# Attention block pipeline of a two-layer trunk: earlier weight splits, one slot for a short block's maps, later low parts, earlier fetches

## The chip, the cores and the metric

One Trainium2 chip, one of its cores. The metric is the device time of one launch in microseconds, the median of several runs. The engines are named as the profile names them: PE (TensorE, matrix products, its weight loads are PEld), DVE (VectorE), ACT (ScalarE), POOL (GpSimd) and SP (SyncE, which here issues every DMA). Each engine takes its own instructions strictly in the order in which they were written, and waits at the first one whose inputs are not there.

## The reference, cut to what matters

Two layers over 1024 tokens of width 1024: a gated short convolution, then causal differential attention with 8 heads of two maps each.

```python
proj = h @ w_in                                   # D -> 4 W: q, k, v, z
logits = einsum('bqhd,bkhd->bhqk', q_blk, k) * scale + bias      # causal, blocks of 128 queries
p = softmax(logits).reshape(bsz, N_DIFF_HEADS, 2, Q_BLOCK, s)
a = p[:, :, 0] - lam * p[:, :, 1]                 # the two maps of a head
o = rmsnorm(einsum('bhqk,bkhe->bqhe', a, v), subln_g) * (1 - lambda_init)
x = x + (o * silu(z)) @ w_out                     # then a final rmsnorm
```

## The kernel before, in words

Products are made from halves: a float32 operand is split into a high part (a rounded copy) and a low part (what is left), and three products of 128x128 by 512 or 256 columns take the place of one. A weight **unit** of 128x1024 is loaded by SP into a raw slot (`wr`, two slots), ACT writes its high part `wh` (L407), POOL subtracts to get its low part `wl` (L408); there are two slots of each, and a raw slot is free again when POOL has subtracted.

The second layer is what the change touches. It runs in 64 **steps**, s = 8h + qb, head h and block qb of 128 queries; the eight steps of a head are a **round** here. In step s, PE computes the scores of block s (`scores`, L612), then the product of one half unit (`half.mm`, L132 for keys, queries and gates, L525 for values), then, at even s, the values of the blocks s-4 and s-3 (`values`, L659). DVE adds the bias and takes the maximum (L615, L617), ACT writes the two maps' exponentials (L619); one step later `differences` subtracts the maps on DVE (L633), ACT and DVE, or for qb >= 5 ACT and POOL (L640), make the 16-bit high and low part, and SP transposes both by DMA (L645) for the value product. The first map lies in a slot of `r_p1` (five slots), the second in one of `r_p2` (three); the second holds the two 16-bit parts, so that it is free again only when its transposition has landed.

The table `plan` says which half unit a step multiplies; `when` gives the step in which a unit is split, as soon as the unit before the last is used up, and `loads` the step in which its raw weights are fetched. Inside a step the order is: loads, evictions (`evict`), squares of a finished half head, the first part of the last half unit's eviction (`first`), scores, splits of weights (`preps`), the product, `differences` of the block before, the rest.

After a head's half is done, its 512 norm factors are stored to HBM as single elements (`store_factors`, L688) and fetched back, spread over all partitions, as `rb` (`fetch_factors`, L692, a tile of 128x512 in one slot `dgl`); POOL multiplies them and the gate into the head's output two steps into the next round but one (L494, `Gate.multiply`), and stores that (L496). In the last eight steps `closing` also fetches, scales and splits the output weights (L854 to L856), with the subtraction on DVE; `tail` then does the output projection.

Of the kernel before, what the change touches and what calls it, by code (L numbers as in the profile page):

```python
# [50 lines left out]
def trunk(ctx: ExitStack, tc: tile.TileContext, a: dict, out: bass.AP):  # L51
# [539 lines left out]
    def scores(h, qb):  # L591
# [5 lines left out]
        p1_ = r_p1.tile([P, S], F32, name="p1")  # L597
        p2_ = r_p2.tile([P, S], F32, name="p2")
# [23 lines left out]

    def differences(h, qb):

        hd = heads[h]
        L = (qb + 1) * P
        p1_, p2_, st = hd.pop(("p", qb))

        cs = sm.tile([P, 2], F32, tag="cs", bufs=2, name="cs")
        V.reciprocal(out=cs, in_=st)  # L630
        V.tensor_scalar(out=cs[:, 1:2], in0=cs[:, 1:2], scalar1=st[:, 0:1], scalar2=nlam, op0=ALU.mult, op1=ALU.mult)
        V.tensor_scalar(out=cs[:, 0:1], in0=cs[:, 0:1], scalar1=cc, scalar2=None, op0=ALU.mult)
        V.scalar_tensor_tensor(out=p1_[:, :L], in0=p2_[:, :L], scalar=cs[:, 1:2], in1=p1_[:, :L],  # L633
                               op0=ALU.mult, op1=ALU.add)
        p16 = p2_.bitcast(F16)
        ah, al = p16[:, :L], p16[:, L:2 * L]
        if qb >= 5:
            A.activation(out=p1_[:, :L], in_=p1_[:, :L], func=AF.Copy, scale=cs[:, 0:1])
            A.activation(out=ah, in_=p1_[:, :L], func=AF.Copy)
            G.tensor_tensor(out=al, in0=p1_[:, :L], in1=ah, op=ALU.subtract)  # L640
        else:
            A.activation(out=ah, in_=p1_[:, :L], func=AF.Copy, scale=cs[:, 0:1])  # L642
            V.scalar_tensor_tensor(out=al, in0=p1_[:, :L], scalar=cs[:, 0:1], in1=ah, op0=ALU.mult, op1=ALU.subtract)  # L643
        at = p1_.bitcast(F16).rearrange("p (b q) -> p b q", q=P)
        dma(out=at[:, :2 * qb + 2, :], in_=p16[:, :2 * L], transpose=True)  # L645
        hd["at", qb] = at
# [42 lines left out]

    def fetch_factors(h, half):  # L690
        rbs[h, half] = rb = sm.tile([P, 512], F32, tag="dgl", name="rb")
# [29 lines left out]
    add("q", 1, (4, 7))  # L721
    add("k", 1, (5, 6))
# [12 lines left out]
    loads, preps, when = {}, {}, {}  # L735
    for i, (_, _, u) in enumerate(units):
        when[i] = max(units[i - 2][1] + 1, when[i - 1], -1) if i > 1 else -9
        preps.setdefault(when[i], []).append(u)
        loads.setdefault(max(when[i - 2] + 1, -1) if i > 1 else -9, []).append(u)

    fetches = {}
    for t, half in plan.items():
        if isinstance(half, Gate) and half.h < L7:
            fetches.setdefault(t - 1 + half.half, []).append((half.h, half.half))

    def step(s, score=True):
        h, qb = divmod(s, 8)
        for u in loads.get(s, ()):
            u.load()
# [5 lines left out]
        if s % 4 == 3 and 0 <= s - 7:  # L755
            ph, pqb = divmod(s - 7, 8)
            sqo = ph, pqb // 4, head_squares(ph, pqb // 4)
        if last:
            last.first()
        half = plan.get(s)  # L760
# [86 lines left out]
    def prep_w(d):  # L847
# [8 lines left out]
        V.tensor_tensor(out=wl, in0=wr, in1=f(wh), op=ALU.subtract)  # L856
# [80 lines left out]
    def layer1():  # L937
        prelude()
        for s in range(NS):
            step(s)  # L940
# [3 lines left out]

    def closing(s):

        if s == 56:
            n = r_q.n
            q0, q1, q2, q3, spare = (r_q.tags[(n + 1 + i) % 5] for i in range(5))
            r_raw.append(Ring(sl, [spare, (wp, "wr0"), (wp, "wr1")]))  # L950
            pb = [r_p2.tags[(r_p2.n + i) % 3] for i in (1, 2, 0)]
            wtags.update({2: r_v.tags[:2], 3: (q0, q1), 4: (r_k.tags[1], pb[0]), 5: (q2, q3), 6: r_k.tags[2:],
                          7: (pb[1], pb[2])})
            fetch_w(2)
        elif s == 57:
            prep_w(2)
        elif s == 59:
            fetch_w(3)
            fetch_w(0)
        elif s == 60:  # L960
            prep_w(3)
            prep_w(0)
        elif s == 61:
            yh[:], yl[:] = new_x()
            fetch_y(0, 0)
            fetch_y(2, 0)
        elif s == 62:
            splits(0, 0)
            fetch_w(1)
            fetch_y(4, 0)  # L970
        elif s == 63:
            splits(2, 0)
            differences(L7, 7)
            for d in (0, 2, 3):
# [131 lines left out]
```

## Time and profile before

| | us |
|---|---|
| median of 3 runs (1184.52 to 1190.43) | 1188.75 |
| the profiled execution's own time | 1192.76 |
| its span, first to last instruction | 1191.0 |
| first layer and the start of the second, to the scores of step 0 | 490.9 |
| rounds 0 to 6 (steps 0 to 55) | 477 |
| round 7 (steps 56 to 63) to the end of its products, and the tail | 223 |
| PE busy | 1090.4 |

The steps can be found in the timeline by PE's score products (L612): four instructions for a block under 4, eight for the others. A stretch between two such places is a step or a round, and the view of busy time by stretches gives for it, after its bounds and length, the busy time of PE, PEld, DVE, ACT and POOL (with the number of instructions) and the clock that PE was granted (1.00 is 2.4 GHz, 0.50 is 1.2 GHz), then the DMA engines' share and GB/s. A matmul's end is modelled, so that PE's busy time in a stretch at half clock is longer for the same work.

### The profile page before, as it was taken

The page shows a single profiled execution, that of the slowest core. Times are in us where ns is not written, and L with a number is a line of the kernel's source. Part 1 is how long each engine was busy: PE and PEld are TensorE (multiplying, and loading weights), DVE is VectorE, ACT ScalarE, POOL GpSimd, SP SyncE. Part 2 cuts the span into 40 slices and gives each one's busy share as a digit, 9 for nine tenths or more (in the row PEclk, how much of TensorE's full clock was granted, in tenths as well). Part 3 has the DMA queues.
Part 4 walks back from the last instruction along what each step waited for, and adds up shares of the span by engine and source line. Part 5 has one row for each costly group of instructions (what it writes and reads, how often), then busy time and mean ns, then how long its engine had stood idle before and what let it go on. Part 6 is the DMA issues. An engine that isn't in the chain of part 4 may idle for free.

```text
span 1191.0 us, 15198 instructions
## 1 busy us (share of the span) xinstructions
PE 1090.4 (92%) x5900; PEld 916.7 (77%) x5900; DVE 598.1 (50%) x951; ACT 437.1 (37%) x715; POOL 517.2 (43%) x315
## 2 busy tenths in 40 slices
PE   8899999999999999798799898989989895878886
PEld 6678888888888888776678787888878785666686
DVE  6563323222324223678485766767676564762522
ACT  3221111111112322447254563746455362544421
POOL 7553433424424443454246564545546461131143
PEclk9899999999999999889799998999999897888898
DMA  5211111111113341434467685886767774453132
GB/s 180 86 55 54 53 39 50 54 53 38 52 53 100 131 145 71 97 92 105 67 84 119 111 155 83 134 131 97 121 92 141 104 143 63 113 136 107 62 107 80
DMA packets 123192, 111.86 MB, mean 94 GB/s; under 512 B 88128, under 2 KB 95984, under 8 KB 123120
## 3 DMA queue, kind: packets, MB, share of 16 engines
q1 hardware_dynamic: 123120, 110.90, 42.4%
q8 instruction: 46, 0.75, 0.3%
q14 instruction: 26, 0.21, 0.1%
HBM read 67.82 MB, written 11.59 MB: 67 GB/s over the span
## 4 chain that ended last, share of the span: by engine, by line
PE 59%; DVE 11%; POOL 8%; issue 7%; DMA 7%; ACT 6%; SPq 1%; POOLq 0%; DVEq 0%; ACTq 0%
PE big L132 35%; PE mm L132 18%; POOL wl L408 3%; PE sc L612 2%; DVE nm L617 2%; DMA wr<-in_w_in 2%; DMA p<-p 2%; PE av L659 2%; DMA wr<-in_w_out 2%; DVE p L633 1%; PE mm L525 1%; DMA qt<-qt 1%; POOL o L494 1%; POOL qt L465 1%; ACT wh L407 1%
## 5 line engine op out<-in xcount | busy, mean ns | idle before, releaser
L132 PE MATMUL mm<-xh,wl 128*128 128x512 f32 (+1 forms) x424 | 170.0, 401 | 20.3 <-POOL wl L408 20.3
L120 POOL TENSOR_TENSOR wl<-wr,wh 128x1024 fp32r<-128x1024 f32 x37 | 90.1, 2435 | 215.9 <-ACT wh L119 215.9
L132 PE MATMUL mm<-xl,wh 128*128 128x512 f32 (+1 forms) x424 | 169.2, 399 | 4.7 <-DVE xl L826 4.7
L132 PE MATMUL mm<-xh,wh 128*128 128x512 f32 (+1 forms) x424 | 169.3, 399 | 2.2 <-ACT xh L825 2.0
L408 POOL TENSOR_TENSOR wl<-wr,wh 128x1024 fp32r<-128x1024 f32 x40 | 95.6, 2392 | 129.5 <-ACT wh L407 129.0
L132 PE MATMUL big<-xh,wh 128*128 128x512 f32 x472 | 147.2, 391 | 2.2 <-DVE cr L289 2.2
L119 ACT ACTIVATE wh<-wr 128x1024 fp32r<-128x1024 f32 x37 | 39.2, 1061 | 294.4 <-PE big L132 293.6
L132 PE MATMUL big<-xh,wl 128*128 128x512 f32 x472 | 146.8, 391 | 0.0
L132 PE MATMUL big<-xl,wh 128*128 128x512 f32 x472 | 146.4, 390 | 0.0
L619 ACT ACTIVATE p<-sc,nm 128x256 f32<-128x256 f32 (+7 forms) x128 | 94.4, 740 | 90.1 <-DVE nm L617 33.6
L132 PEld LDWEIGHTS mm<-xh,wl 128*128 128x128 f32 x424 | 83.9, 198 | 41.9 <-POOL wl L408 25.3
L612 PE MATMUL sc<-kt,qt 128*128 128x512 f32 (+2 forms) x384 | 91.6, 374 | 16.6 <-ACT p L619 13.0
L132 PEld LDWEIGHTS big<-xh,wh 128*128 128x128 f32 x472 | 89.0, 189 | 21.0 <-issue 2.6
L132 PEld LDWEIGHTS big<-xl,wh 128*128 128x128 f32 x472 | 88.9, 188 | 18.6
L132 PEld LDWEIGHTS big<-xh,wl 128*128 128x128 f32 x472 | 88.9, 188 | 18.4
L132 PEld LDWEIGHTS mm<-xl,wh 128*128 128x128 f32 x424 | 83.9, 198 | 22.4 <-DVE xl L826 6.9
L132 PEld LDWEIGHTS mm<-xh,wh 128*128 128x128 f32 x424 | 83.9, 198 | 19.0 <-ACT xh L825 3.5
L617 DVE TENSOR_REDUCE nm<-sc 128x2 f32<-128x256 f32 (+5 forms) x96 | 92.0, 958 | 3.3
L612 PEld LDWEIGHTS sc<-kt,qt 128*128 128x128 f32 x384 | 67.4, 201 | 27.7 <-ACT p L619 16.1
L525 PE MATMUL mm<-wl,xh 128*128 128x256 f32 x256 | 75.4, 294 | 7.0 <-POOL wl L408 7.0
L643 DVE SCALAR_TENSOR_TENSOR p<-p,cs,p 128x128 f16<-128x128 f32 (+4 forms) x40 | 46.9, 1174 | 68.6 <-ACT p L642 68.1
L525 PE MATMUL mm<-wh,xh 128*128 128x256 f32 x256 | 75.5, 295 | 0.8 <-DVE tq L460 0.6
(186 smaller groups left out, 2038.8 us busy)
## 6 DMA issues: line engine op xcount, KB each, us to landing
wr<-in_w_in SPq DMA_DIRECT2D x53, 512.0 KB, 3.7
wr<-in_w_out SPq DMA_DIRECT2D x16, 512.0 KB, 4.7
wr<-in_w_v SPq DMA_DIRECT2D x16, 512.0 KB, 5.1
qt<-qt SPq DMA_DIRECT2D x32, 256.0 KB, 7.5
xr<-in_xT SPq DMA_DIRECT2D x15, 512.0 KB, 4.3
x2d<-x SPq DMA_DIRECT2D x8, 512.0 KB, 2.8
kt<-lo SPq DMA_DIRECT2D x32, 128.0 KB, 9.5
rb<-rrd SPq DMA_DIRECT2D x14, 256.0 KB, 5.4
```

The lines of the kernel that those rows point to most:

```text
L119: A.activation(out=wh, in_=wr, func=AF.Copy)
L120: G.tensor_tensor(out=wl, in0=wr, in1=f(wh), op=ALU.subtract)
L132: T.matmul(ps[:, o:o + n], lhsT=w[:, s], rhs=r[k][:, t:t + n], start=(k == 0 and r is rh and w is wh), stop=(k == KC - 1 and w is wl))
L407: A.activation(out=self.wh, in_=self.wr, func=AF.Copy)
L408: G.tensor_tensor(out=self.wl, in0=self.wr, in1=f(self.wh), op=ALU.subtract)
L465: G.tensor_tensor(out=qt[own[m], 1, :], in0=tq[own[m]], in1=f(qt)[own[m], 0, :], op=ALU.subtract)
L525: T.matmul(self.pts[tp][:, i, :], lhsT=x[k][:, ts], rhs=w[:, kk], start=(k == 0 and i == 0 and x is xh and w is wh), stop=(k == KC - 1 and ...
L612: T.matmul(sc[:, i, c0:c1_], lhsT=qt[:, var, ts], rhs=kt[:, c0:c1_], start=(var == 0), stop=(var == 1))
L617: V.tensor_reduce(out=nm[:, ms], in_=sc[:, :, :L], axis=AX, op=ALU.max, negate=True)
L619: A.activation(out=(p1_, p2_)[m][:, :L], in_=sc[:, i, :L], func=AF.Exp, bias=nm[:, m:m + 1], accum_out=st[:, m:m + 1])
L643: V.scalar_tensor_tensor(out=al, in0=p1_[:, :L], scalar=cs[:, 0:1], in1=ah, op0=ALU.mult, op1=ALU.subtract)
L659: T.matmul(av[:, qi * P:(qi + 1) * P], lhsT=v[:, kb, es], rhs=at[:, r, :], start=(kb == 0 and r == 0 and v is vh), stop=(kb == qb and v is ...
```

## The change

It changes no arithmetic and no shape; the order of PE's instructions stays the same but for the swap of two units in round 0. It does five things:

1. A unit whose split falls in the step right ahead of its use (`soon`) is split first in that step (`early`), before evictions and scores; the raw loads move behind `first` in the step, and a load that follows an early split stands in the same step and not in the next. In round 0 the keys of head 1 come before its queries.
2. Blocks with qb < 4 put both maps into one `r_p1` slot (two halves of 512), and use no `r_p2` slot.
3. For qb >= 5 POOL's low part and the transposition (`turn`) are put off into the next step, ahead of `first`.
4. The factors of both halves of a head are fetched in the same step, one step ahead of the gate's first product, into one `r_p2` slot.
5. In the last round the output weights and finished heads are fetched ahead of the step (`opening`) and not after it, and POOL takes the subtraction of three of the weights from DVE.

```diff
@@ scores
-        p1_ = r_p1.tile([P, S], F32, name="p1")
-        p2_ = r_p2.tile([P, S], F32, name="p2")
+        if qb < 4:
+            p12 = r_p1.tile([P, 2, 512], F32, name="p1")
+            p1_, p2_ = p12[:, 0, :], p12[:, 1, :]
+        else:
+            p1_ = r_p1.tile([P, S], F32, name="p1")
+            p2_ = r_p2.tile([P, S], F32, name="p2")
@@ differences
-            G.tensor_tensor(out=al, in0=p1_[:, :L], in1=ah, op=ALU.subtract)
...
+        def turn():
+            if qb >= 5:
+                G.tensor_tensor(out=al, in0=p1_[:, :L], in1=ah, op=ALU.subtract)
+            at = p1_.bitcast(F16).rearrange("p (b q) -> p b q", q=P)
+            dma(out=at[:, :2 * qb + 2, :], in_=p16[:, :2 * L], transpose=True)
+            hd["at", qb] = at
+        if qb < 5 or (h, qb) == (0, 7):
+            turn()
+        else:
+            turns.append(turn)
@@ fetch_factors
-        rbs[h, half] = rb = sm.tile([P, 512], F32, tag="dgl", name="rb")
+        if h == L7 - 1:
+            rb = sm.tile([P, 512], F32, tag="dgl", name="rb")
+        elif half:
+            rb = rb2[0][:, 1, :]
+        else:
+            rb2[:] = [r_p2.tile([P, 2, 512], F32, name="rb")]
+            rb = rb2[0][:, 0, :]
+        rbs[h, half] = rb
@@ tables
-    add("q", 1, (4, 7))
-    add("k", 1, (5, 6))
+    add("k", 1, (4, 6))
+    add("q", 1, (5, 7))
...
-        preps.setdefault(when[i], []).append(u)
-        loads.setdefault(max(when[i - 2] + 1, -1) if i > 1 else -9, []).append(u)
+        soon[i] = when[i] > 0 and use == when[i] + 1
+        (early if soon[i] else preps).setdefault(when[i], []).append(u)
+        loads.setdefault(max(when[i - 2] + (not soon[i - 2]), -1) if i > 1 else -9, []).append(u)
...
-        if isinstance(half, Gate) and half.h < L7:
+        if isinstance(half, Gate) and half.h < L7 - 1:
+            fetches.setdefault(t - 1 - half.half, []).append((half.h, half.half))
+        elif isinstance(half, Gate) and half.h < L7:
             fetches.setdefault(t - 1 + half.half, []).append((half.h, half.half))
@@ step
-        for u in loads.get(s, ()):
-            u.load()
+        for u in early.get(s, ()):
+            u.prep()
...
+        for fn in turns:
+            fn()
+        turns.clear()
         if last:
             last.first()
+        for u in loads.get(s, ()):
+            u.load()
@@ prep_w
-    def prep_w(d):
+    def prep_w(d, eng=V):
-        V.tensor_tensor(out=wl, in0=wr, in1=f(wh), op=ALU.subtract)
+        eng.tensor_tensor(out=wl, in0=wr, in1=f(wh), op=ALU.subtract)
@@ layer1, closing
+            if s >= 56:
+                opening(s)
             step(s)
...
-    def closing(s):
+    def opening(s):
...
             fetch_w(2)
-        elif s == 57:
-            prep_w(2)
         elif s == 59:
             fetch_w(3)
             fetch_w(0)
-        elif s == 60:
-            prep_w(3)
-            prep_w(0)
         elif s == 61:
-            yh[:], yl[:] = new_x()
             fetch_y(0, 0)
             fetch_y(2, 0)
         elif s == 62:
+            fetch_w(1)
+        elif s == 63:
+            fetch_y(4, 0)
+
+    def closing(s):
...
+        elif s == 57:
+            prep_w(2, G)
+        elif s == 60:
+            prep_w(3, G)
+            prep_w(0, G)
...
         elif s == 62:
             splits(0, 0)
-            fetch_w(1)
-            fetch_y(4, 0)
```

The order of instructions shows it at two places. The first is POOL's queue in round 4 (from step 32 on), `wl` being a weight's low part, `p` a map's low part, `o` the gate and factor products. Before:

```order
L408 TENSOR_TENSOR wl<-wr,wh 128x1024
L640 TENSOR_TENSOR p_6406<-p_6405,p_6406 128x1024
L494 TENSOR_TENSOR o<-o,rb 128x512
L494 TENSOR_TENSOR o<-o,th 128x512
L408 TENSOR_TENSOR wl<-wr,wh 128x1024
L494 TENSOR_TENSOR o<-o,rb 128x512
L494 TENSOR_TENSOR o<-o,th 128x512
L408 TENSOR_TENSOR wl<-wr,wh 128x1024
L678 TENSOR_TENSOR rr<-rr,neghalf 128x4
L408 TENSOR_TENSOR wl<-wr,wh 128x1024
```

And now:

```order
L408 TENSOR_TENSOR wl<-wr,wh 128x1024
L652 TENSOR_TENSOR p_7105<-p_7104,p_7105 128x1024
L494 TENSOR_TENSOR o<-o,rb 128x512
L494 TENSOR_TENSOR o<-o,th 128x512
L408 TENSOR_TENSOR wl<-wr,wh 128x1024
L494 TENSOR_TENSOR o<-o,rb 128x512
L494 TENSOR_TENSOR o<-o,th 128x512
L408 TENSOR_TENSOR wl<-wr,wh 128x1024 x2
L691 TENSOR_TENSOR rr<-rr,neghalf 128x4
```

The queue up to the keys' split (the third `wl`) stands as it stood; the queries' split, which stood behind the factor's root `rr`, now follows the keys' directly.

The second is SP's queue of the same places, from a round's step 6 into the next round: `rb` is the fetch of factors, `rrd` their store, `wr` raw weights, a DMA_TRANSPOSE of 12, 14 and 16 the blocks 5, 6 and 7 of a head. Before:

```order
L645 DMA_TRANSPOSE p_6250<-p_6251 128x12x128
L697 DMA bias<-stripd 128x2x256
L437 DMA kt<-lo 64x512 x2
L645 DMA_TRANSPOSE p_6316<-p_6317 128x14x128
L692 DMA rb<-rrd 128x512
L403 DMA wr<-in_w_v 128x1024
L466 DMA qt<-qt 64x2x512 x2
L645 DMA_TRANSPOSE p_6405<-p_6406 128x16x128
L688 DMA rrd<-rr 128x4x1
```

And now:

```order
L719 DMA bias<-stripd 128x2x256
L654 DMA_TRANSPOSE p_6227<-p_6228 128x12x128
L437 DMA kt<-lo 64x512
L403 DMA wr<-in_w_v 128x1024
L437 DMA kt<-lo 64x512
L714 DMA rb<-rrd 128x512 x2
L654 DMA_TRANSPOSE p_6293<-p_6294 128x14x128
L466 DMA qt<-qt 64x2x512 x2
L701 DMA rrd<-rr 128x4x1
L654 DMA_TRANSPOSE p_6388<-p_6389 128x16x128
```

Both fetches of factors now stand ahead of block 6's transposition, and block 7's transposition behind the single-element store and no longer ahead of it.

## Rows read from the trace of the kernel before

**Rows 1.** Rounds 1 to 6: length, engines' busy time, PE's granted clock.

```profile
554.90:625.60 70.70, 56.87 (x366) 49.32 (x366) 48.18 (x86) 35.31 (x67) 29.09 (x18) 0.88 0.53 79
625.60:695.20 69.60, 64.91 (x415) 55.97 (x414) 43.96 (x81) 36.41 (x65) 37.38 (x23) 0.95 0.71 126
695.20:763.70 68.50, 64.31 (x415) 55.41 (x415) 49.13 (x90) 37.43 (x70) 35.51 (x24) 0.95 0.71 105
763.70:829.30 65.60, 61.62 (x414) 53.64 (x413) 43.37 (x81) 34.99 (x63) 36.48 (x23) 1.00 0.81 129
829.30:897.80 68.50, 63.94 (x415) 54.97 (x414) 48.82 (x90) 38.46 (x72) 36.40 (x24) 0.98 0.68 113
897.80:967.90 70.10, 64.64 (x415) 55.79 (x414) 43.43 (x81) 35.33 (x63) 36.71 (x23) 0.95 0.72 121
```

**Rows 2.** Waits of PE over the span: total us, times, longest.

```profile
PE mm L132 <- POOL wl L408: 20.3, 9, 5.2
PE sc L612 <- ACT p L619: 13.0, 8, 5.4
PE cps L157 <- ACT sqo L668: 12.0, 1, 12.0
```

**Rows 3.** Timeline, POOL and PE, step 36: start, us, idle before, releaser.

```profile
795.16 1.30 POOL L494 TENSOR_TENSOR o<-o,rb 128x512 f32<-128x512 f32 x1 [9.26 <-DMA rb<-rrd]
...
797.96 2.34 POOL L408 TENSOR_TENSOR wl<-wr,wh 128x1024 fp32r<-128x1024 f32 x1
...
800.36 0.50 PE L132 MATMUL mm<-xh,wl 128*128 128x512 f32 x1 [3.37 <-POOL wl L408]
```

**Rows 4.** Line view: the stores of factors, and transpositions in rounds 2 to 6.

```profile
L688 SPq DMA_DIRECT2D rrd<-rr x14: 520/578/935, 571.7 to 1021.6; - x14
...
DMA to landing us min/median/max: 9.9/10.0/11.0
...
L645 SPq DMA_TRANSPOSE p<-p x40: 1177/1332/3923, 630.3 to 961.1; - x40
...
DMA to landing us min/median/max: 3.1/5.2/13.4
```

**Rows 5.** Timeline, ACT and PE, steps 11 and 12.

```profile
588.24 0.69 ACT L619 ACTIVATE p<-sc,nm 128x512 f32<-128x512 f32 x1 [8.94 <-DMA p<-p]
...
589.07 0.69 PE L612 MATMUL sc<-kt,qt 128*128 128x384 f32 x1 [5.41 <-ACT p L619]
```

**Rows 6.** Timeline, ACT and PE, step 59.

```profile
995.88 1.15 ACT L854 ACTIVATE wr<-wr,gsub 128x1024 f32<-128x1024 f32 x1 [15.33 <-DMA wr<-in_w_out]
...
1009.33 1.87 PE L157 MATMUL cps<-ones_r,sqo 128*128 128x1 f32 x8 [12.01 <-ACT sqo L668]
```

**Rows 7.** Busy time by stretches: steps 10, 12, 36, 59, 60 and 61.

```profile
557.25:575.26 18.01, 12.62 (x106) 11.87 (x103) 11.65 (x17) 9.28 (x22) 12.17 (x7) 0.81 0.55 89
582.83:601.30 18.47, 10.53 (x45) 8.38 (x45) 7.95 (x16) 6.14 (x11) 7.14 (x5) 0.72 0.33 93
795.20:806.00 10.80, 7.43 (x43) 5.93 (x42) 6.92 (x15) 5.36 (x10) 8.60 (x6) 1.00 0.48 140
990.70:1011.00 20.30, 8.29 (x40) 6.81 (x37) 10.94 (x15) 6.64 (x11) 5.01 (x3) 0.73 0.26 62
1011.00:1021.40 10.40, 10.20 (x43) 8.37 (x43) 7.83 (x19) 5.07 (x11) 2.22 (x2) 0.70 0.46 147
1021.40:1030.50 9.10, 7.07 (x35) 5.60 (x32) 5.79 (x8) 5.93 (x7) 0.61 (x1) 1.00 0.22 33
```

**Rows 8.** Timeline, SP and PE, round 4: block 7's transposition and its value product.

```profile
776.59 2.46 SPq L645 DMA_TRANSPOSE p<-p  x1
...
785.03 2.69 PE L659 MATMUL av<-p,vt 128*128 128x128 f16 x45
```

**Rows 9.** Timeline, DVE: L643 of 384 columns beside a POOL split, and alone.

```profile
590.56 2.29 DVE L643 SCALAR_TENSOR_TENSOR p<-p,cs,p 128x384 f16<-128x384 f32 x1 [9.31 <-ACT p L642]
...
1013.15 0.62 DVE L643 SCALAR_TENSOR_TENSOR p<-p,cs,p 128x384 f16<-128x384 f32 x1 [1.04 <-ACT p L642]
```

More of the change, by code (lines that the diff above doesn't have):

```diff
@@ L621, in scores @@
         hd["p", qb] = p1_, p2_, st
+    turns = []
     def differences(h, qb):
@@ L643, in differences @@
             V.scalar_tensor_tensor(out=al, in0=p1_[:, :L], scalar=cs[:, 0:1], in1=ah, op0=ALU.mult, op1=ALU.subtract)
-        at = p1_.bitcast(F16).rearrange("p (b q) -> p b q", q=P)
-        dma(out=at[:, :2 * qb + 2, :], in_=p16[:, :2 * L], transpose=True)
-        hd["at", qb] = at
+        def turn():
[8 more added lines that the diff above has]
+            turns.append(turn)
     def values(h, g):
@@ L688, in store_factors @@
                 dma(out=rrd[h, half].rearrange("(b p) -> p b", p=P), in_=rr)
+    rb2 = []
     def fetch_factors(h, half):
-        rbs[h, half] = rb = sm.tile([P, 512], F32, tag="dgl", name="rb")
+        if h == L7 - 1:
[6 more added lines that the diff above has]
+        rbs[h, half] = rb
         dma(out=rb, in_=rrd[h, half].unsqueeze(0).partition_broadcast(P))
@@ L733, in trunk @@
     units.sort(key=lambda x: x[0])
-    loads, preps, when = {}, {}, {}
-    for i, (_, _, u) in enumerate(units):
+    loads, preps, early, when, soon = {}, {}, {}, {}, {}
+    for i, (use, _, u) in enumerate(units):
         when[i] = max(units[i - 2][1] + 1, when[i - 1], -1) if i > 1 else -9
-        preps.setdefault(when[i], []).append(u)
-        loads.setdefault(max(when[i - 2] + 1, -1) if i > 1 else -9, []).append(u)
+        soon[i] = when[i] > 0 and use == when[i] + 1
+        (early if soon[i] else preps).setdefault(when[i], []).append(u)
+        loads.setdefault(max(when[i - 2] + (not soon[i - 2]), -1) if i > 1 else -9, []).append(u)
     fetches = {}
     for t, half in plan.items():
-        if isinstance(half, Gate) and half.h < L7:
+        if isinstance(half, Gate) and half.h < L7 - 1:
+            fetches.setdefault(t - 1 - half.half, []).append((half.h, half.half))
+        elif isinstance(half, Gate) and half.h < L7:
             fetches.setdefault(t - 1 + half.half, []).append((half.h, half.half))
@@ L943, in layer1 @@
         tail()
-    def closing(s):
+    def opening(s):
         if s == 56:
-            n = r_q.n
-            q0, q1, q2, q3, spare = (r_q.tags[(n + 1 + i) % 5] for i in range(5))
+            q0, q1, q2, q3, spare = (r_q.tags[(r_q.n + 3 + i) % 5] for i in range(5))
             r_raw.append(Ring(sl, [spare, (wp, "wr0"), (wp, "wr1")]))
-            pb = [r_p2.tags[(r_p2.n + i) % 3] for i in (1, 2, 0)]
-            wtags.update({2: r_v.tags[:2], 3: (q0, q1), 4: (r_k.tags[1], pb[0]), 5: (q2, q3), 6: r_k.tags[2:],
-                          7: (pb[1], pb[2])})
+            wtags.update({2: r_v.tags[:2], 3: (q0, q1), 5: (q2, q3), 6: r_k.tags[2:]})
             fetch_w(2)
-        elif s == 57:
-            prep_w(2)
         elif s == 59:
@@ L967, in closing @@
         elif s == 62:
+            fetch_w(1)
+        elif s == 63:
+            fetch_y(4, 0)
+    def closing(s):
+        if s == 56:
+            pb = [r_p2.tags[(r_p2.n + i) % 3] for i in (1, 2, 0)]
+            wtags.update({4: (r_k.tags[1], pb[0]), 7: (pb[1], pb[2])})
+        elif s == 57:
[3 more added lines that the diff above has]
+            prep_w(0, G)
+        elif s == 61:
+            yh[:], yl[:] = new_x()
+        elif s == 62:
             splits(0, 0)
-            fetch_w(1)
-            fetch_y(4, 0)
         elif s == 63:
@@ L973, in closing @@
             differences(L7, 7)
+            for fn in turns:
+                fn()
+            turns.clear()
             for d in (0, 2, 3):
```

## The prediction

> **What bounds the kernel now.** I read the page's shares first: PE is busy for 1090.4 of a span of 1191.0 us, so PE sets the time and only what PE waits for, or does at half clock, can be won. Next I read the list of PE's waits. The three that the change can touch are PE waiting for POOL's low weight parts, 20.3 us in 9 times, for ACT's exponentials at the scores, 13.0 in 8, and once 12.0 for ACT's squares [rows 2]. Third come the rounds of the second layer as stretches [rows 1]. Round 4 shows what a round's work costs at full speed: PE busy 61.62 us at a granted clock of 1.00. The other rounds from 2 to 6 have the same number of matmuls and last up to 70.1 us, and in them the clock is 0.95 to 0.98 and busy time 2.3 to 3.3 us more: after a wait PE is granted 1.2 GHz for a while. So a wait is paid twice, as idle time and as slower work behind it.
>
> Where is it lost? In rounds 2 to 6 most of the excess stands in one step, 8h+4, where the product with the next head's keys begins. The timeline of step 36 shows the chain: POOL stands 9.26 us at its product with `rb`, whose fetch has not landed; behind it in POOL's queue is the keys' split, which starts at 797.96, and PE waits 3.37 us for it [rows 3]. The fetch is late because of what is ahead of it on the DMA side: the store of 512 single elements takes 9.9 to 11.0 us to land, and transpositions issued behind it up to 13.4, where 3.1 is the least and 5.2 the median [rows 4].
>
> Round 1 loses it elsewhere. In step 12 ACT stands 8.94 us before an exponential, because the `r_p2` slot that it writes still waits for an older transposition, and PE 5.41 [rows 5]; the step takes 18.47 us with 10.53 busy at clock 0.72, while step 36, the same block number, needs PE for 7.43 at 1.00 [rows 7]. Round 7 loses it at step 59: ACT stands 15.33 us at the first output weight, whose fetch was issued too late, and PE 12.01 [rows 6].
>
> **Sum, part by part.** All durations are of one execution with span 1191.0 and time 1192.76, which is 4.0 above the median of 1188.75; I subtract from 1192.76 and then take off the 4.0.
>
> *Factors ahead, low parts a round's step later, weights first (edits 1, 3, 4), rounds 2 to 6.* Both fetches now stand ahead of block 6's transposition and, with it, ahead of the store; the order of SP's queue shows it. Then POOL does not stand at `rb`, and the keys' split, with ACT's high part now at the head of its step, is done when PE comes. The five rounds last 69.6 + 68.5 + 65.6 + 68.5 + 70.1 = 342.3 us. With no wait and full clock they would last 5 x 61.62 = 308.1. The most that can be won is 34.2, or 6.8 a round [rows 1].
>
> Something is given back. Block 7's transposition now stands behind the single-element store. Before, it was issued at 776.59 and its value product began at 785.03, in which block 6 comes first; block 7's share of the 2.69 us begins after about half, at 786.3 [rows 8]. Issued at the same time, but behind a store that is still landing, it takes between 3.1 and 13.4 us [rows 4]: it lands at 779.7 to 790.0, and PE waits 0 to 3.7 a round. I take 2, between the ends, since the transpositions behind the store lie near the upper one but the store is now issued some us earlier. That is 10 for five rounds, and 24.2 is left (bounds 34.2 - 18.5 = 15.7 and 34.2).
>
> The moved issues cost SP little in themselves (fetches and transpositions are as many as before). The early split puts ACT's high part (an ACT pass over 128x1024, 1.15 [rows 6]) and POOL's subtraction (2.34 [rows 3]) ahead of evictions and scores. On ACT it is queued ahead of work that PE needs one step on, so that PE's product of the same step covers it; without the cover it would cost 1.15 for each of 27 early splits, 31 us. I count nothing, since ACT is busy for 35 to 38 us of a round's 66 to 70 [rows 1]; the range's upper end takes in the larger part of the 31.
>
> *One slot for short blocks (edit 2), round 1.* The wait of ACT for the slot in step 12 goes, since block 4 is the first of a head that uses `r_p2`, and three slots then serve four blocks and the factors instead of eight blocks. Step 12 falls to 7.43: 18.47 - 7.43 = 11.0 [rows 7]. Step 10 takes 18.01 with 12.62 busy at 0.81; its 5.4 idle stem from several causes, of which the slots are one. I take 2, bounds 0 and 5.4 plus 3.4 of slow clock (about a quarter of 12.62), that is 8.8 [rows 7]. Sum 13.0.
>
> *Opening and the subtraction on POOL (edit 5), round 7.* The weights are issued a step earlier, so step 59 falls to its busy time: 20.30 - 8.29 = 12.0. Step 60 is 10.40 at clock 0.70, which lies behind that wait; at full clock it would save about 6.2 x 1/2 = 3.1 (0.6 of it at half clock is 6.2, and half of that goes). Step 61 is 9.10 with 7.07 busy, 2.0 [rows 7]. That is 17.1, of which I keep back 1.0 for three subtractions on POOL (2.34 each against idle time of POOL, which is busy 5.01 of 20.30 in step 59 [rows 3, 7]). Sum 16.1, bounds 8 and 17.1.
>
> *Round 0.* The swap of keys and queries lets a wait of PE for POOL go and may put one in its place; a wait of that list is 20.3/9 = 2.3 [rows 2]. I take 0, bounds -2.3 and +2.3.
>
> Total 24.2 + 13.0 + 16.1 = 53.3. The execution's 1192.76 becomes 1139.5, the median 1188.75 - 53.3 = 1135.45: **1135 us**.
>
> A rule speaks against moving subtractions from DVE to POOL and POOL's work closer to DVE's. What the trace shows: DVE's subtraction of 384 columns took 2.29 us while POOL split a weight, and 0.62 elsewhere with POOL idle [rows 9], so 1.67 more. The Trainium skill, page "SBUF — State Buffer", section "Who interferes with whom", says that a DVE instruction with two inputs in SBUF contends with a GpSimd instruction that reads SBUF; by that rule, the row agrees, and what it makes of the time is the third rival.
>
> **Rivals.**
>
> (a) *All is hidden.* Block 7's transposition lands in time, and steps 10 and 59 to 61 fall to their busy time: 34.2 + 11.0 + 7 + 17.1 is about 70, so 1119. For it: POOL is busy 36 us of 66 a round and has room [rows 1]. Against: five kinds of DMA share the queue around the store.
>
> (b) *Half is given back.* The stall moves to the value product of blocks 6 and 7, a wait of 3.7 with its slow stretch (64.9 - 61.6 = 3.3 [rows 1]) each round, 7.0 and no better than before: of rounds 2 to 6 nothing is left, 53.3 - 24.2 = 29, so 1160. For it: the store's 10 us, which the change moves but does not shorten [rows 4].
>
> (c) *DVE is held by POOL.* If two splits a round coincide anew with a subtraction on PE's path, 2 x 1.67 x 7 rounds = 23 us are lost [rows 9]: 1135 + 23 = 1158. Against: the splits are as many as before, and move by part of a step.
>
> (d) *It does not do what it says.* POOL still waits for `rb` since it is now one slot of a ring that a transposition must leave first; round 1 and 7 give a few us at most: 1186.
>
> (e) *Slower: SP stands at the factors' fetch.* The fetch needs an `r_p2` slot that is free only when block 5's transposition has landed, and that is issued a step later than before. Everything that SP has behind it waits: block 6's transposition, the queries, the store, block 7's transposition. If that landing takes 13.4 us and not 5.2 [rows 4], all this is issued 8.2 later, and block 7's lands at 776.59 + 8.2 + 13.4 = 798.2 against 786.3 [rows 4, 8]: 11.9 of wait and 3.3 of slow clock, 15.2 a round where 6.8 was lost. Five rounds cost 42, rounds 1 and 7 give 29: 1189 + 13 = 1202. It decides from a landing of about 12 us on, where the loss exceeds 6.8 + 29/5 = 12.6 a round. Against: block 5's transposition is issued before any store of its round.
>
> **How the numbers follow.** Forecast (1122 to 1150) 0.50; (a) 0.13; (b) 0.14; (c) 0.08; (d) 0.06; (e) 0.09. The likeliest gives 1135. From 1115 to 1168 lie the forecast, (a), (b) and (c), 0.85, of which some must be taken off since their ends are not sharp; the bounds of the terms (15.7 + 11 + 8 - 2.3 = 32, so 1156, and 70) lie inside. About 0.5%, 6 us, is what a measurement of this kernel can tell from no change: forecast, (a), (b), (c) are faster by more, 0.85; (d) is within, 0.06; (e) is slower, 0.09.
>
> **What would show it.** Right: POOL's wait for `rb` (9.26 [rows 3]) is gone, and with it most of PE's 20.3 for POOL's low weights; rounds 2 to 6 last 62 to 65 each; ACT's 8.94 and 15.33 [rows 5, 6] are gone. Block 7's part of the value product shows 0 to 4 of wait. Wrong: PE waits over 4 us a round at the value product of blocks 6 and 7 (b); subtractions on DVE of 2 us or more beside POOL's splits and PE waiting for them (c); long semaphore waits on SP at the fetch (e); rounds 2 to 6 still near 68 (d).

## The result

The changed kernel takes 1123.18 us (median of 4 runs, 1118.79 to 1127.33) against 1187.49 for the kernel before on the same chip: 0.946 of it, interval 0.941 to 0.950. Measured once more beside later experiments it was 0.945 (0.941 to 0.949). The profiled execution has a span of 1122.7 us against 1191.0.

The forecast was 1135, with 1115 to 1168 as its range. The size and the sign came out; the runs below show that two of the mechanisms in the sum were not the ones that paid.

Rounds 1 to 6 after the change, in the columns of [rows 1]:

```profile
552.40:613.10 60.70, 53.16 (x367) 47.42 (x367) 45.06 (x86) 35.22 (x67) 30.84 (x19) 0.92 0.54 94
613.10:674.10 61.00, 61.00 (x414) 53.80 (x414) 45.31 (x81) 35.09 (x63) 37.35 (x23) 1.00 0.71 135
674.10:735.50 61.40, 61.37 (x415) 53.83 (x415) 49.14 (x90) 38.04 (x70) 36.55 (x23) 1.00 0.73 124
735.50:798.10 62.60, 61.10 (x414) 53.74 (x413) 46.92 (x82) 34.97 (x62) 38.17 (x23) 1.00 0.72 131
798.10:859.30 61.20, 61.20 (x416) 53.99 (x415) 47.76 (x91) 38.64 (x71) 37.55 (x23) 1.00 0.63 126
859.30:920.90 61.60, 61.13 (x414) 53.77 (x414) 44.68 (x81) 34.88 (x63) 37.29 (x23) 1.00 0.78 134
```

From round 2 on a round is as long as PE's work in it, but for 0.5 us in round 6 and 1.5 in round 4, at a granted clock of 1.00. The five rounds from 2 to 6 take 307.8 where they took 342.3. Of PE's three waits of [rows 2] the first and the third are gone, and of the second's 13.0 us 1.9 are left; the longest are now for transpositions:

```profile
PE av L672 <- DMA p<-p: 10.3, 4, 7.5
...
PE sc L616 <- ACT p L623: 1.9, 2, 1.6
```

Of those 10.3 us, 7.45 stand at one place, step 10, where block 7 of the first head comes late. The first line is that wait. The three stretches under it are step 10 (from the start of step 9, as in [rows 7], which is 0.8 us earlier), step 12 and step 59, in the columns of [rows 7]:

```profile
570.90 2.31 PE L672 MATMUL av<-p,vt 128*128 128x128 f16 x20 [7.45 <-DMA p<-p]
```

```profile
554.74:573.40 18.66, 11.12 (x105) 10.70 (x103) 10.72 (x17) 9.40 (x22) 11.95 (x6) 0.81 0.69 118
582.36:589.68 7.32, 7.32 (x44) 6.18 (x44) 6.36 (x18) 3.61 (x7) 5.39 (x5) 1.00 0.51 100
944.52:951.79 7.27, 7.27 (x40) 6.15 (x38) 5.12 (x10) 3.19 (x7) 0.93 (x1) 1.00 0.55 185
```

Steps 12 and 59 have fallen to PE's work. Step 10 has won nothing. In the kernel before PE waited there for a low part of the values' weights, the longest wait of this line:

```profile
PE mm L525 <- POOL wl L408: 7.0, 2, 5.3
```

Those 5.3 us are gone, and the 7.45 for block 7's transposition stand in their place.

By place, from the two traces: round 0 won 2.6 us, round 1 10.1, rounds 2 to 6 34.4, and round 7 with the tail 21.3, together 68.4. The terms of the prediction were 0, 13.0, 24.2 and 16.1. Which edit won it, the traces alone can't tell, since five edits came together.

### The profile page after: what moved, and what is told of

It is laid out like the page before. It is cut to its first block, busy times and chain, and to the rows that moved or that the text cites. A ratio compares the mean times of both kernels' runs of the same rounds, so it can differ in the third digit from the quotient of the medians.

```text
span 1122.7 us, 15168 instructions
## 1 busy us (share of the span) xinstructions
PE 1062.3 (95%) x5900; PEld 901.2 (80%) x5900; DVE 595.9 (53%) x948; ACT 438.1 (39%) x715; POOL 529.9 (47%) x318
## 4 chain that ended last, share of the span: by engine, by line
PE 77%; DVE 7%; DMA 5%; POOL 5%; ACT 3%; issue 2%; SPq 0%; POOLq 0%; DVEq 0%; ACTq 0%
PE big L132 37%; PE mm L132 25%; PE sc L616 5%; PE mm L525 5%; DMA p<-p 3%; PE av L672 3%; DVE p L639 1%; PE cps L157 1%; POOL p L652 1%; POOL wl L408 1%; DVE nm L621 1%; POOL qt L465 1%; DMA xr<-in_xT 1%; ACT p L644 1%; POOL w3l L254 0%
## 5 line engine op out<-in xcount | busy, mean ns | idle before, releaser
L132 PE MATMUL mm<-xh,wh 128*128 128x512 f32 (+1 forms) x424 | 163.3, 385 | 4.2 <-ACT xh L855 4.1
L132 PE MATMUL mm<-xl,wh 128*128 128x512 f32 (+1 forms) x424 | 163.8, 386 | 2.9 <-DVE xl L856 2.9
L132 PE MATMUL mm<-xh,wl 128*128 128x512 f32 (+1 forms) x424 | 162.6, 384 | 0.0
L132 PEld LDWEIGHTS mm<-xh,wh 128*128 128x128 f32 x424 | 80.2, 189 | 19.9 <-ACT xh L855 5.6
L132 PEld LDWEIGHTS mm<-xl,wh 128*128 128x128 f32 x424 | 80.2, 189 | 18.8 <-DVE xl L856 4.7
L132 PEld LDWEIGHTS mm<-xh,wl 128*128 128x128 f32 x424 | 80.3, 189 | 15.6
L616 PE MATMUL sc<-kt,qt 128*128 128x512 f32 (+2 forms) x384 | 86.2, 360 | 4.7 <-issue 2.0
L616 PEld LDWEIGHTS sc<-kt,qt 128*128 128x128 f32 x384 | 64.4, 193 | 13.0 <-ACT p L623 3.2
L525 PE MATMUL mm<-wh,xl 128*128 128x256 f32 x256 | 74.4, 290 | 0.0
```

The costliest lines, as they stand in the source:

```text
L132: T.matmul(ps[:, o:o + n], lhsT=w[:, s], rhs=r[k][:, t:t + n], start=(k == 0 and r is rh and w is wh), stop=(k == KC - 1 and w is wl))
L525: T.matmul(self.pts[tp][:, i, :], lhsT=x[k][:, ts], rhs=w[:, kk], start=(k == 0 and i == 0 and x is xh and w is wh), stop=(k == KC - 1 and ...
L616: T.matmul(sc[:, i, c0:c1_], lhsT=qt[:, var, ts], rhs=kt[:, c0:c1_], start=(var == 0), stop=(var == 1))
```

## The experiments

The theories tested first: **A**, the prediction's, that the late fetch of factors held POOL and through it PE, and that the slots held step 12; and **B**, that the order on POOL and ACT (edits 1 and 3) did it. All ratios are to the kernel before on the same chip in the same set.

### Edit 4 undone: the fetch is not the cause

```diff
-        elif half:
-            rb = rb2[0][:, 1, :]
-        else:
-            rb2[:] = [r_p2.tile([P, 2, 512], F32, name="rb")]
-            rb = rb2[0][:, 0, :]
+        rbs[h, half] = rb = sm.tile([P, 512], F32, tag="dgl", name="rb")
...
-            fetches.setdefault(t - 1 - half.half, []).append((half.h, half.half))
+            fetches.setdefault(t - 1 + half.half, []).append((half.h, half.half))
```

> The changed kernel with edit 4 undone: the two halves' factors are fetched one after the other into the one slot of the kernel before, in the old steps. Theory A (the late second fetch is what held POOL, and through it the keys' split and PE at step 8h+4; all of the 34.5 us that rounds 2 to 6 gained hangs on it): POOL waits for rb again, 5 to 10 us in each of rounds 2 to 6, rounds 2 to 6 last 66 to 70 each, and the time is 1145 to 1160. Theory B (weights split first in a step and low parts a step later are what keeps POOL's queue ahead; the fetch is hidden anyway): rounds stay at 61 to 63 and the time is 1120 to 1130.

Measured: 0.940 (0.937 to 0.944), no slower than the changed kernel. Theory A falls. What makes this instructive is that POOL's wait is there again, 6.2 to 8.9 us once in each of rounds 2 to 6. Round 4, POOL around the keys' split, start, length, idle before and its releaser, to be read beside [rows 3]:

```profile
751.06 2.41 POOL L408 TENSOR_TENSOR wl<-wr,wh 128x1024 fp32r<-128x1024 f32 x1
761.83 1.29 POOL L494 TENSOR_TENSOR o<-o,rb 128x512 f32<-128x512 f32 x1 [8.37 <-DVE cs L636]
763.20 1.49 POOL L494 TENSOR_TENSOR o<-o,th 128x512 f32<-128x512 f32 x1
764.65 5.05 POOL L408 TENSOR_TENSOR wl<-wr,wh 128x1024 fp32r<-128x1024 f32 x2
```

```profile
766.10:773.30 7.20, 7.20 (x43) 6.07 (x43) 5.90 (x13) 3.87 (x8) 6.82 (x5) 1.00 0.67 176
```

POOL stands 8.37 us before the factor product, nearly as long as the 9.26 of [rows 3] (that the profile names DVE as the last releaser doesn't matter here; the fetched row landed at 761.8). But it comes free 26.1 us after the round's start (735.7) and not 31.5 after it (795.2 - 763.7). The keys' split ends in time, and step 36, the second view above, is all PE work. (Steps 28 and 44 do lose, 9.1 and 9.0 us for 7.3, with PE waiting 1.5 and 1.4 for DVE, but rounds 2 to 6 together take 309.3 us, as long as in the second profile of the changed kernel.) An idle engine with a row of its own in the chain was not the cause; the question was what set the time at which its wait ended.

### Edit 3 undone: the place of the store

```diff
-        if qb < 5 or (h, qb) == (0, 7):
+        if True:
             turn()
```

> The changed kernel with edit 3 undone: low parts and transpositions of the long blocks in their own step again. Theory A (the fetch is the cause): block 7's transposition stands ahead of the single-element store again, PE's waits at the value product of blocks 6 and 7 (1.5, 0.5 and 0.9 us in three rounds) go; 1119 to 1126. Theory B (POOL's order matters: a long low part ahead of the keys' split delays it, and ACT's second pass delays the low part): PE waits 2 to 3 us in a round with a slow clock behind; 1135 to 1150.

Measured: 0.954 (0.952 to 0.957), 10 to 11 us slower than the changed kernel; theory B's side. Its SP queue in round 4 shows a thing that I had passed over in the trace of before. First the kernel without edit 3, then the kernel before, then the changed one (start and length of SP's instruction, in the three the same round):

```profile
760.39 1.97 SPq L654 DMA_TRANSPOSE p<-p  x1
762.41 1.00 SPq L701 DMA_DIRECT2D rrd<-rr  x1
763.46 0.51 SPq L403 DMA_DIRECT2D wr<-in_w_in  x1
764.08 11.41 SPq L654 DMA_TRANSPOSE p<-p  x1
```

```profile
779.10 0.59 SPq L688 DMA_DIRECT2D rrd<-rr  x1
779.74 0.51 SPq L403 DMA_DIRECT2D wr<-in_w_in  x1
780.36 1.19 SPq L645 DMA_TRANSPOSE p<-p  x1
781.65 9.52 SPq L496 DMA_DIRECT2D yd<-o  x1
791.23 0.42 SPq L692 DMA_DIRECT2D rb<-rrd  x1
```

```profile
744.87 1.08 SPq L701 DMA_DIRECT2D rrd<-rr  x1
748.12 1.90 SPq L654 DMA_TRANSPOSE p<-p  x1
750.07 1.04 SPq L403 DMA_DIRECT2D wr<-in_w_in  x1
751.22 1.17 SPq L654 DMA_TRANSPOSE p<-p  x1
752.49 0.52 SPq L496 DMA_DIRECT2D yd<-o  x1
```

In the kernel before, SP itself stands 9.52 us in the issue of an output store, which elsewhere takes 0.3 to 0.5, and the second fetch is next in its queue: it is issued at 791.23 for that reason. In the other rounds SP doesn't stand, and the fetch, issued 3.1 us behind the store, lands with what else is behind it (in round 3 it is issued at 713.52, and POOL is free at 727.13). Without edit 3 SP stands 11.41 at a transposition, the raw weights issued ahead of it land 15.6 us after their issue, and ACT, which now has a split at the head of its step, stands with it:

```profile
779.16 1.06 ACT L407 ACTIVATE wh<-wr 128x1024 fp32r<-128x1024 f32 x1 [12.05 <-DMA wr<-in_w_in]
```

In both kernels this is the second or third issue behind the store of single elements. What holds SP in it the profile does not say. In the changed kernel the store comes 9.4 us after the round's start (15.4 in the kernel before, 14.3 without edit 3), ahead of block 7's transposition and not behind it, and SP stands in no issue (the longest of a transposition takes 3.4). In rounds 2 to 6 what is issued next behind that store still lands 7.0 to 11.9 us after its issue, but the store itself is issued 6 to 9 us earlier in the round. This made a new theory, **C**: the single-element store holds SP and all DMA behind it, and the change won by moving it to a better place.

### Edit 1 undone, and edits 2 and 4 undone

```diff
-        for u in early.get(s, ()):
-            u.prep()
+        for u in loads.get(s, ()):
+            u.load()
...
-        soon[i] = when[i] > 0 and use == when[i] + 1
-        (early if soon[i] else preps).setdefault(when[i], []).append(u)
+        preps.setdefault(when[i], []).append(u)
```

> The changed kernel with edit 1 undone: units are split after the scores again, raw loads at the head of a step, queries ahead of keys in round 0. Theory A (the late fetch is the cause): POOL comes to each split in time anyway, PE waits 0 to 1 us for low parts, round 0 goes back by its 2.6 us; 1123 to 1131. Theory B (the early split is the cause): PE waits for POOL's low parts in most rounds as before (20.3 us over the span with slow clock behind); 1140 to 1160.

Measured: 0.970 (0.968 to 0.972), 28 to 30 us slower than the changed kernel: by far the largest share of any edit. But PE waits for low parts only 13.6 us in 8 times, where it waited 27.3 in 11 in the kernel before (both kinds of product together), and no longer in step 36. Round 4, SP again:

```profile
768.19 1.00 SPq L701 DMA_DIRECT2D rrd<-rr  x1
769.29 1.48 SPq L403 DMA_DIRECT2D wr<-in_w_in  x1
771.07 10.37 SPq L654 DMA_TRANSPOSE p<-p  x2
```

With the raw loads at the head of the step, one stands between the store and block 7's transposition, SP stands 9.1 of these 10.37 us at the latter, and PE waits 2.83 for it in the value product.

The slots, priced against the kernel with edit 4 undone:

```diff
-        if qb < 4:
-            p12 = r_p1.tile([P, 2, 512], F32, name="p1")
-            p1_, p2_ = p12[:, 0, :], p12[:, 1, :]
-        else:
-            p1_ = r_p1.tile([P, S], F32, name="p1")
-            p2_ = r_p2.tile([P, S], F32, name="p2")
+        p1_ = r_p1.tile([P, S], F32, name="p1")
+        p2_ = r_p2.tile([P, S], F32, name="p2")
```

> The changed kernel with edits 2 and 4 undone (short blocks take a slot of each ring, factors fetched late). Against u4_fetch_late, which undoes 4 alone, it prices the slots. Theory A (the wait of the exponential for an r_p2 slot in step 12 was the slots'): 9 to 12 us more than u4_fetch_late, all of it in round 1. Theory B (step 12's wait came from its transpositions standing behind the store, which the other edits have moved): within 3 us of u4_fetch_late.

Measured: 0.944 (0.941 to 0.946) against 0.940 (0.937 to 0.944), 3.8 us apart by the medians, with intervals that overlap. Step 12 keeps its whole gain with the old slots, and so theory A's price for them, 11 us, falls too:

```profile
582.03:589.39 7.36, 7.36 (x45) 6.20 (x44) 6.75 (x19) 4.26 (x8) 5.29 (x5) 1.00 0.39 109
```

In that kernel ACT still waits for transpositions before its exponentials (32.8 us in 9 times over the span, 24.6 in the kernel before), but up to step 62 PE waits for an exponential in step 60 alone (1.05 us). Round 1 is as long as with the new slots (60.2 us for 60.5). Edit 2 was not undone alone: edit 4's fetch uses the slot that it frees, and no run has that fetch with the old slots.

### The store itself: 128 pieces for 512

Theory C is tested by taking away the store's cost and as little else as possible. The factors go out as four neighbouring elements for each partition, and POOL reads the fetched row through a view in the matching order:

```diff
-                dma(out=rrd[h, half].rearrange("(b p) -> p b", p=P), in_=rr)
+                dma(out=rrd[h, half].rearrange("(p b) -> p b", p=P), in_=rr)
...
+            rb = rbs.pop((self.h, self.half)).rearrange("x (p b) -> x b p", b=4)
+            ov = o.rearrange("x (b p) -> x b p", b=4)
+            G.tensor_tensor(out=ov, in0=ov, in1=rb, op=ALU.mult)
```

> The kernel before, with one thing changed: the 512 factors are stored as 128 pieces of four neighbouring elements (16 bytes) and not as 512 single ones, and POOL reads the fetched row in the matching order. Theory C (the single-element store fills the DMA rings, holds SP's next issues some 9 us and everything behind it 10 to 13 us; all that the changed kernel won in rounds 2 to 6 is that it keeps the others away from it): the store lands in under 5 us, SP's 9.5 us stand at the output store of step 34 goes, transpositions behind it take 4 to 6, rounds 2 to 6 fall to 61.5 to 64, and the time to 0.965 to 0.985 of the kernel before. Theory D (the order of ACT and POOL is what counts, the store is a bystander): rounds 2 to 6 stay at 65 to 70 and the ratio at 0.99 to 1.00.

> The changed kernel with edit 3 undone (transpositions at once, 0.954 of the kernel before) and the store in 128 pieces. Theory C: deferring the transpositions only served to get the store out earlier; with a short store the ratio is that of the changed kernel, 0.940 to 0.948, SP has no stand of 11 us, rounds 3 to 6 at 61 to 63. Theory D: POOL's and ACT's order in steps 8h+3 and 8h+4 costs the same whatever the store: 0.951 to 0.957.

> The changed kernel with edit 1 undone (splits last, loads at the head of a step, 0.970 of the kernel before) and the store in 128 pieces. Theory C: 0.945 to 0.955, since most of the 30 us that undoing edit 1 cost was SP standing 9 us behind the store at block 7's transposition, with PE waiting for what came late. Theory D: the late split itself costs it, PE waiting for POOL's low parts; 0.965 to 0.972.

> The changed kernel with the store in 128 pieces. Theory C: little is left to win, since the changed kernel has the store out of the way; PE's waits at the value product (1.5, 0.5 and 0.9 us and slow clock behind) go, 0.940 to 0.946. Theory D: the same as the changed kernel, 0.944 to 0.948. A time over 0.95 would say that the reading of the row in another order costs POOL something, which would blur the three other kernels of this set.

| | store as it was | store in 128 pieces |
|---|---|---|
| kernel before | 1 | 0.966 (0.962 to 0.971) |
| changed kernel | 0.946 (0.941 to 0.950) | 0.936 (0.933 to 0.940) |
| edit 3 undone | 0.954 (0.952 to 0.957) | 0.938 (0.935 to 0.942) |
| edit 1 undone | 0.970 (0.968 to 0.972) | 0.954 (0.950 to 0.958) |

In the kernel before, this alone wins 39 us of the 64 that the five edits win. The landing of the stores, of the line that had 9.9/10.0/11.0 in [rows 4], and the same issues of SP in round 4:

```profile
DMA to landing us min/median/max: 1.7/2.7/3.9
```

```profile
759.76 0.57 SPq L690 DMA_DIRECT2D rrd<-rr  x1
760.39 0.42 SPq L403 DMA_DIRECT2D wr<-in_w_in  x1
760.92 1.82 SPq L647 DMA_TRANSPOSE p<-p  x1
762.84 0.53 SPq L498 DMA_DIRECT2D yd<-o  x1
763.42 0.42 SPq L694 DMA_DIRECT2D rb<-rrd  x1
```

The store lands in 2.7 and not 10.0, the transposition behind it at 765.5, 4.5 after its issue and not 13.4, and SP doesn't stand. (POOL pays a little for its view: its product with the row takes 1.62 us and not 1.34 in the median, 14 times.) With the short store edit 3 is worth nothing that can be told (0.938 against 0.936): it had served to bring the store forward. Edit 1 keeps the larger part of its worth: undoing it cost 0.024 of the kernel before, some 29 us, and costs 0.018, 21 us, with the short store (0.954 against 0.936). So the ratio fell into theory C's range, but that most of those 30 us hung on the store is not borne out. And the five edits together still win 0.030, 36 us, where the store is short: of their 64 us, 28 hang on the store and 36 do not. And the kernel before keeps an excess in every second round only:

```profile
616.40:677.60 61.20, 61.20 (x414) 53.69 (x413) 46.32 (x81) 34.45 (x62) 36.99 (x23) 1.00 0.60 125
677.60:744.30 66.70, 63.70 (x415) 54.86 (x414) 51.50 (x90) 37.66 (x71) 36.75 (x24) 0.97 0.53 117
744.30:805.90 61.60, 61.38 (x415) 53.77 (x414) 45.51 (x81) 34.55 (x63) 36.78 (x23) 1.00 0.63 131
```

In rounds 2 to 6 two causes can be told apart: the kernel before takes 342.3 us and with the short store 318.0; the changed kernel with the short store takes 305.5, and 318.1 when edit 1 is undone. So the short store alone wins 24 of the 34 us that were won there, and what it leaves is edit 1's. The two overlap: with the store as it was, undoing edit 1 costs 26 us there (334.2 for 307.8), with the short store 13.

The last kernel of the set landed somewhat below its expectation's lower end (0.936 for 0.940), so the changed kernel still paid for the store, some 11 us by the ratios and 4 to 6 by the spans of the profiled executions. A part of it are PE's waits for transpositions at the value product (1.5 to 1.7 us in steps 34, 50 and 58 of its second profile).

### What else edit 1 does: POOL's split beside DVE's subtraction

Most of the excess of the odd rounds stands in steps 28 and 44 (11.0 and 11.2 us for 7.3). It is there too with edit 1 undone and the short store (11.2 and 11.3). That kernel's steps 27 and 28, DVE, POOL and PE:

```profile
706.73 2.81 DVE L641 SCALAR_TENSOR_TENSOR p<-p,cs 128x384 f32<-128x384 f32 x1
...
710.75 0.22 DVE L692 TENSOR_SCALAR rr<-cps,ec 128x4 f32<-128x4 f32 x1
```

```profile
706.75 2.37 POOL L408 TENSOR_TENSOR wl<-wr,wh 128x1024 fp32r<-128x1024 f32 x1 [3.58 <-ACT wh L407]
```

```profile
711.02 0.58 PE L555 MATMUL nps<-sq,ones_r 128*128 128x256 f32 x1 [2.08 <-DVE rr L692]
```

The subtraction of 384 columns took 2.81 us where 0.62 is its length alone [rows 9]; it began 0.02 before POOL's split and ended 0.42 behind its end. DVE's factor `rr` comes later by that, and PE waits 2.08. The Trainium skill, page "SBUF — State Buffer", section "Who interferes with whom", says that a DVE instruction with two inputs in SBUF contends with a GpSimd instruction that reads SBUF; these rows agree. Over the span DVE's two subtractions of a block, of the maps and for the low part, took 129.9 us in this kernel (80.9 and 48.9), and 112.6 (78.1 and 34.5) with edit 1 and the short store: the early split moves POOL's work off them. The five edits together hardly do. The kernel before took 114.4 (67.4 and 46.9) and the changed kernel 111.9 (80.0 and 31.9): what the second subtraction lost the first gained, but in steps 8 to 62 none of PE's waits over 0.25 us is for DVE. So the prediction's third rival had the rule right, and its loss did not come.

To separate that from "a late split is late", the splits were put behind the subtraction of the maps in their step:

```diff
-        for u in preps.get(s, ()) if s else ():
-            u.prep()
...
         if 0 <= s - 1 < NS - 1:
             differences(*divmod(s - 1, 8))
+        for u in preps.get(s, ()) if s else ():
+            u.prep()
```

> Edit 1 undone and the store in 128 pieces (0.954 of the kernel before), with one more thing moved: the splits stand behind the subtraction of the maps in the step and not ahead of it. Theory E (what is left of edit 1's worth is that POOL's split no longer runs beside DVE's subtractions: there DVE's 128x384 ones took 2.3 and 2.8 us where 0.6 is the length without it, and PE waited 2.1 us in step 28 with a slow clock behind): DVE's second subtractions fall from 48.9 us over the span to under 40, steps 28 and 44 from 11.2 to 7.3 to 8.5, the ratio to 0.940 to 0.948. Theory F (a split that comes late in a step is late for PE, whatever it runs beside): PE waits for low parts more than the 7 us of that kernel, steps 28 and 44 stay above 10, and the ratio at 0.952 to 0.965.

Measured: 0.977 (0.975 to 0.980), slower than with the clash. Both theories have a part. The clash of step 28 is gone: the second subtractions fall to 26.6 us, and step 28 from 11.2 to 8.1. (The splits now run beside the first subtraction of block 7, which takes 3.10 us in step 32 where 1.28 is its least.) But PE now waits for the split itself, and from round 2 on the first step of a round takes 12.6 to 12.8 and not 8.1 to 8.4:

```profile
PE mm L132 <- POOL wl L408: 23.0, 16, 1.7
PE mm L132 <- ACT wh L407: 6.8, 6, 1.1
```

```profile
752.80:765.40 12.60, 9.76 (x62) 7.71 (x62) 5.07 (x8) 6.92 (x11) 10.56 (x6) 0.86 0.48 120
```

Neither of the two late places is good: in the middle of a step the splits run beside DVE's subtraction and PE waits behind that, at its end they come too late for PE. At the head of the step, edit 1, PE has neither wait. That PE's wait in step 28 comes from the clash alone is made likely by this, not shown by a kernel that has the clash removed and nothing else.

### The last round, and the empty steps

The last set had the changed kernel itself beside it as a yardstick.

> The changed kernel itself once more, beside the other three of this set on one chip: 0.940 to 0.950 of the kernel before by either theory. It is the yardstick for them.

It measured 0.945 (0.941 to 0.949).

Edit 5 undone (output weights and heads fetched behind their step, DVE subtracts them):

```diff
-    def opening(s):
+    def closing(s):
...
+        elif s == 57:
+            prep_w(2)
         elif s == 59:
             fetch_w(3)
             fetch_w(0)
+        elif s == 60:
+            prep_w(3)
+            prep_w(0)
```

> The changed kernel with edit 5 undone: output weights and heads fetched behind their step, DVE subtracts them. Theory G (step 59's 12 us wait came from the late issue): step 59 takes 12 to 20 us and not 7.3, the ratio is 10 to 17 us, 0.009 to 0.014, above the changed kernel of this set. Theory C (it came from the store ahead of the fetch in the rings, which is out of the way now): step 59 takes 7.3 to 9 and the ratio is within 0.004 of it; the kernel before with the short store, whose step 59 took 12.7, speaks for something between.

Measured: 0.952 (0.949 to 0.955), 8 us above the yardstick by the two ratios, 10.5 by the medians and 13 by the spans of the profiled executions. Steps 59, 60 and 61 there:

```profile
944.40:955.80 11.40, 8.33 (x40) 6.87 (x37) 9.50 (x14) 4.44 (x9) 5.07 (x3) 0.89 0.12 34
955.80:965.30 9.50, 9.32 (x42) 7.68 (x43) 7.47 (x18) 5.07 (x11) 1.47 (x2) 0.77 0.47 142
965.30:975.20 9.90, 7.11 (x36) 5.65 (x34) 7.20 (x9) 5.94 (x7) 0.82 (x1) 1.00 0.24 46
```

Step 59 takes 11.4, between the 7.3 of the changed kernel and the 20.3 of [rows 7], which gives both theories a share: of the 13 us in that step 4 hang on the early issue, and 9 on the other four edits. That most of these 9 are the store's is borne out by the kernel before with the short store, where step 59 takes 12.7 and not 20.3. The rest of edit 5's worth lies in the three steps behind.

Last, a version meant to beat both: the short store, and the second head's products moved into the two steps 8 and 9, which have none.

```diff
+            e = 2 * (h == 1)
-            add_v((h + 1) // 2, (h + 1) % 2, (s0, s0 + 1))
-            add("k", h + 1, (s0 + 2, s0 + 4))
-            add("q", h + 1, (s0 + 3, s0 + 5))
+            add_v((h + 1) // 2, (h + 1) % 2, (s0 - e, s0 + 1 - e))
+            add("k", h + 1, (s0 + 2 - e, s0 + 4 - e // 2))
+            add("q", h + 1, (s0 + 3 - e, s0 + 5 - e // 2))
```

> The changed kernel with the store in 128 pieces and the second head's products moved two steps ahead into steps 8 and 9, which have none (value halves in 8 and 9, keys 10 and 13, queries 11 and 14). Theory H (step 10 waits 5 to 7 us for block 7's transposition because PE runs ahead through two empty steps): steps 8 to 15 take 57 to 60 and step 10 loses its wait; 2 to 6 us better than the short store alone, 0.931 to 0.936. Rival (the empty steps give the wait elsewhere: the same work has to pass ACT, DVE and POOL): round 1 stays at 57 to 61 and the ratio at 0.935 to 0.940.

Measured: 0.938 (0.935 to 0.941), the same as the short store alone (0.936). Step 10 fell from 15.8 to 12.1 us, but round 1 took 57.5 after 57.7, and step 16 grew from 7.9 to 9.5. The rival is right: the wait is given to the steps behind. The short store on the changed kernel is the best of them, about 1% below the changed kernel (0.936 for 0.945 and 0.946) and 6% below the kernel before.

## Why the prediction held, and where it did not

- **What bounds the kernel.** Right: PE's waits, many with a slow clock behind them. Not each is paid twice: round 4 of the kernel before has the 3.37 us of [rows 3] and a clock of 1.00 [rows 1]. The bound of a round, 61.62 us, was reached within 0.1 in the mean (307.8 for 308.1 in five rounds).
- **Rounds 2 to 6, 24.2 forecast, 34.4 measured.** The ceiling was right, the 10 kept back was not: block 7's transposition, now behind the store, landed 10.5 us after its issue at 748.12, near the upper bound as assumed, but PE waited only 1.5 in round 4 and 0.5 in one other (in the second profile 1.5 in two rounds of the five), where 2 a round was taken. The middle between two bounds was put on a step that is covered in most rounds.
- **The mechanism of that term failed.** The step was that both fetches now stand ahead of the store, and that POOL therefore does not stand at `rb`. Undoing the fetch costs nothing, and the wait comes back without harm. The term had put edits 1, 3 and 4 together, and 1 and 3 earned it. What the prediction did name, the 10 us of the store and what lands late behind it [rows 4], was the larger cause, since the short store alone wins 24 of the 34 us, and the early split was the other; it said that the change moves the fetch past the store, and the runs say that it moves the store past the transposition and the loads. That the size came out is in part luck: it was taken from the ceiling of the rounds, which is the same whatever takes the waits away. Rival (b) had the store moved and not shortened; it was that, and it cost little, because the same waits then fell where nobody was waiting.
- **Round 1, 13.0 forecast, 10.1 measured.** Step 12 fell by the 11 us forecast, but not for the slots' sake: it keeps the gain with the old slots, the short store alone gives it too (7.4 us in the kernel before with it), and with the new slots and edit 1 undone the step takes 16.2, with PE waiting 5.8 for DVE. Step 10's 2 were not won; without step 9 its 17.2 became 17.9, with the wait of 7.45 for block 7's transposition.
- **Round 7, 16.1 forecast, 21.3 measured.** Step 59 won 13.1 for 12.0, step 60 3.1 for 3.1, step 61 2.3 for 2.0; step 62 (2.6) was not priced, and no loss by POOL's subtractions shows. Of step 59, 9 us do not hang on edit 5.
- **Round 0, 0 forecast, 2.6 measured**, beyond the bound of 2.3 by little.
- **Rivals.** (a), all hidden at 1119, came nearest. (c) did not come: DVE's subtractions are held by POOL nearly as much as before, but PE does not wait for them. (d) did not come: in rounds 2 to 6 POOL waits for `rb` nowhere. (e) did not come: in no round does SP stand at the factors' fetch for long. (By (e)'s own figures its loss exceeds 12.6 a round from a landing of 10.8 us on, and not 12.)

## What to carry to other kernels

A wait that stands in the chain and ends last shows where time is lost, not what loses it: ask what set the moment at which it ended, and look at the issuing queue too, where one instruction of 9.5 us among others of 0.5 is easily passed over. Before reordering around a slow transfer, try to make the transfer itself cheap; a store of 512 scattered elements turned into 128 pieces won 39 us where five edits won 64, in two places of the code. And when edits are priced together, the sum can be right for the wrong reasons, so undo them one at a time.

## What the runs showed of the hardware

- Storing 512 single elements of 4 bytes took 9.9 to 11.0 us to land in the kernel before (three of 14 stores, those whose landing the trace has) and 8.5 to 13.2 in the other kernels with this store; 128 pieces of 16 bytes took 1.7 to 5.2. What the kernel before issued within 2.6 us behind such a store landed 12.1 to 14.5 us after its issue, and 3.8 to 6.2 with the short store.
- In some rounds from 2 to 6 (one of the kernel before, one without edit 3, five without edit 1) SP stood 8.0 to 11.4 us in the issue of a later DMA behind the store of single elements; in the kernel before with the short store no issue in these rounds took over 4.6.
- A DVE subtraction of 128x384 took 0.62 us alone, and 2.29 [rows 9] and 2.81 beside a POOL subtraction of 128x1024, each time until 0.4 us behind POOL's end.
